# Layer 0 of a two-layer trunk: inverting the blocks of a head pair in one pass of eight instead of two passes of four

## The chip, the core and the metric

The kernel runs on one core of a Trainium2 chip. The metric is the device time of one execution in microseconds. The engines of the core are named as in the profile: PE (TensorE, matrix products; its weight loads are listed apart as PEld), DVE (VectorE), ACT (ScalarE), POOL (GpSimd) and SP, which here only issues transfers. Each engine runs its own list of instructions in order. PE alone writes PSUM, and DVE and ACT empty it.

## The reference

A trunk of two layers on 512 tokens of width 1024, in float32. Layer 0 mixes the tokens by two recurrent mixers, layer 1 by block attention. Each layer then has an MLP of width 4096 and a gated addition of a second input. The change lies in the second recurrent mixer of layer 0, which has 8 heads of width 64:

```python
def rwkv7_scan(r, decay, k, v, kk, a):
    def step(state, inp):
        r_t, w_t, k_t, v_t, kk_t, a_t = inp
        sa = jnp.einsum('bhvk,bhk->bhv', state, -kk_t)
        state = (state * w_t[:, :, None, :]
                 + sa[..., None] * (kk_t * a_t)[:, :, None, :]
                 + v_t[..., None] * k_t[:, :, None, :])
        return state, jnp.einsum('bhvk,bhk->bhv', state, r_t)
```

Beside it stands a gated linear recurrence with 4 heads of width 128 (`hgrn2_chunked`: scores inside chunks with decays, a state between chunks). The outputs of both are normalised, gated, joined and multiplied by `w_out`:

```python
    o = jnp.concatenate([o_a, o_b], axis=-1).astype(h.dtype)
    return o @ w_out
```

## The kernel before, in words

Large products are made to near float32 precision from three products of split operands: a weight tile of 128x512 is copied to a rounded upper half (`whi`, ACT, L230) and a remainder (`wlo`, DVE, L231), the activations likewise, and `mm3` issues three matmuls of 128x512 (L238 to L240) for each 128 rows of the sum. These are most of the work of PE, and their PSUM tiles come from the ring `pj` with two buffers. Small products of the recurrent mixers use the rings `pmr` (four buffers) and `pmh` (two).

The mixer of layer 0 goes over four head pairs h of the delta-rule mixer (called RWKV here) and, with the same index, four heads of the gated recurrence (HGRN). For each h the steps run in the order of `ORDER = "AFHBOC"`, by which the program is written; a scheduler then places each engine's instructions, the earliest written first among those that it takes for ready. Steps run by `run` get priority as if written 300 instructions earlier. The matmuls of later steps that are ready fill PE while a chain of small steps waits.

RWKV handles the 512 tokens of a head pair in two halves g of 256 tokens, and each half as four blocks (two groups of 128 tokens by two heads):

- `pre` (per pair): decays, normalised keys, the rows that the products need.
- `p1(h, g)`: triangular products of keys with keys and queries, and transposes.
- `p2(h, g)`: inverse of four unit-triangular blocks of 128 by doubling. Each of five levels is: a product of `n16` with the lower part of `X` (L658), a copy of it from PSUM by ACT to `PP` (L661), two products with `PP` (L658), and two masked copies by DVE into `X` (L663) and `XT` (L664). Then comes one correction step in float32 (L670 to L679) and a product with the values to `MU` (L684, L687).
- `p3(h, g)`: the matrices that carry the state over a chunk (L701 to L712), two products with 64 output rows (L720 and L725), the states one after another (L738, L740) and what they add to the output (L748).
- `tail(h)`: layer norm of the pair's output and its split (`os`).

Step A weaves `p2(h, 0)` with `p3(h-1, 1)`, `p1(h, 1)` and `tail(h-1)`; step C weaves `p2(h, 1)` with `pre(h+1)` and `p3(h, 0)` and then runs `p1(h+1, 0)`. `weave(main, side, ratio)` takes `ratio` steps of the side for each of the main.

HGRN (step H) has, for each head, score products over decays at six levels (L825, then five at L845, each behind a difference on POOL, L837, two exponentials on ACT and two products on DVE, L840 and L841), transposes of the keys (L862), products for the states (L867), the output (L876, L878), its mean square (L285), a reciprocal root in twelve small DVE instructions, its broadcast by PE (L328), and a gate, after which POOL (L892) and ACT (L271) make `os`. Step O multiplies the outputs of head h-1 by their part of `w_out` and adds them to `x` (L935). After the last head this is done for head 3, whose result `x` is scaled and split (`act`, L274 and L275) for the MLP of layer 0. The mean square of `x` is summed by POOL from squares made by ACT (`acc`, `xsq`, L307 and L313).

```python
        for h in range(4):
            for c in ORDER:
                step(c, h)
        out_piece(3)
```

Of the kernel before, what the change touches and what calls it, by code (L numbers as in the profile page):

```python
# [12 lines left out]
F32 = mybir.dt.float32  # L13
F32R = mybir.dt.float32r
F16 = mybir.dt.float16
# [15 lines left out]
ND = (2, 2)  # L31
PD = 1
ORDER = "AFHBOC"
R0, R1 = 1.5, 1.5
OFS = 300
NWARM = 9

P = 128
S = 512
# [140 lines left out]
def trunk(ctx, tc, wts, xT, pT, vecs, lora, cst, lev, seg, rope, out, upto="all", dbg=None, mode=None):  # L180
# [119 lines left out]
    class NormAcc:  # L300
# [1 line left out]
            self.ring, self.t = ring, None  # L302

        def add(self, src, eng="act"):
            sq = nrm.tile([P, S], F32, name="acc") if self.t is None else self.ring()
            if eng == "act":
                A.activation(sq, src, AF.Square)  # L307
            else:
                V.tensor_mul(sq, src, src)
            if self.t is None:  # L310
                self.t = sq
            else:
                G.tensor_add(self.t, self.t, sq)  # L313
# [27 lines left out]
    def weave(main, side, ratio):  # L341
        acc = 0.0
        for _ in main:
            yield
            acc += ratio
            while acc >= 1:
                acc -= 1
                if next(side, 0) is None:
                    yield
        for _ in side:  # L350
            yield

    def chain(*gens):
        for g_ in gens:
            yield from g_


    def layer0_mixer(actp):
# [5 lines left out]
        BZ = [mp.tile([P, 2, 2, 2, P], F32, name=f"BZ{i}") for i in range(2)]  # L364
        GB = mp.tile([P, 4, P], F32, name="GB")
        SB = mp.tile([P, 9, P], F32, name="SB")
        PP = mp.tile([P, 4, P], F16, name="PP")
        early = [BH, KAs, *NAs, *BZ, GB, SB, PP]
        for t in early[:NE]:
            G.memset(t, 0.0)  # L370
# [84 lines left out]
        def E(name="e", bufs=EB, shape=None, dt=F32):  # L455
            return ex.tile(shape or [P, S], dt, name=name, bufs=bufs)
# [53 lines left out]
        def four(lhs, rhs):  # L510
            ps = pmr.tile([P, S], F32, name="pmr")
            for i in range(4):
                T.matmul(ps[:, i * P:i * P + P], lhs(i), rhs(i), start=True, stop=True)
            return ps.rearrange("p (i t) -> p i t", i=4)
# [111 lines left out]
            A.copy(y[:, gs], ps[:, :256])  # L626
            yield

        def p2(hp, g):
            NA, TOK = un[hp, g]  # L630

            n16 = E("n16", 1, [P, 4, P], F16)
            for a in range(2):
                A.copy(n16[:, 2 * a:2 * a + 2, :], NA[:, a, :, 0, :])
            X = E("X", 1, [P, 4, P], F16)
            XT = E("XT", 1, [P, 4, P], F16)
            V.tensor_copy(XT, id16[:, None, :].to_broadcast([P, 4, P]))
            V.copy_predicated(XT[:, :, 1::2], m8[:, 0, None, 1::2].to_broadcast([P, 4, 64]), n16[:, :, 1::2])
            A.copy(X, four(lambda i: XT[:, i, :], lambda i: id16))
            yield  # L640
            for l in range(1, 6):
                H = 1 << l

                def lo(t):
                    return t.rearrange("p i (n u) -> p i n u", u=2 * H)[:, :, :, :H]

                def hi(t):
                    return t.rearrange("p i (n u) -> p i n u", u=2 * H)[:, :, :, H:]

                def mask(i, half):  # L650
                    m = half(m8[:, i:i + 1, :])
                    return m.to_broadcast([P, 4, 64 // H, H])

                def half4(lhs, rhs):
                    ps = pmr.tile([P, S], F32, name="pmr")
                    pv = ps[:, :256].rearrange("p (i n u) -> p i n u", i=4, u=H)
                    for i in range(4):
                        T.matmul(pv[:, i], lhs[:, i, :], rhs[:, i], start=True, stop=True)  # L658
                    return pv

                A.copy(lo(PP), half4(n16, lo(X)))  # L661
                yield
                V.copy_predicated(lo(X), mask(7 + l, lo), half4(XT, lo(PP)))  # L663
                V.copy_predicated(hi(XT), mask(l, hi), half4(PP, hi(XT)))  # L664
                yield
            tt = E("tt", 1, [P, 4, P])
            A.copy(tt, X)
            ps = pmr.tile([P, S], F32, name="pmr")
            for i, (a, h) in enumerate(pk):
                T.matmul(ps[:, i * P:i * P + P], NA[:, a, h, 0, :], tt[:, i, :], start=True, stop=False)  # L670
                T.matmul(ps[:, i * P:i * P + P], id16, id16, start=False, stop=True)
            er = E("er", 1, [P, 4, P], F16)
            V.tensor_sub(er, ps.rearrange("p (i t) -> p i t", i=4), tt)
            yield
            ps = pmr.tile([P, S], F32, name="pmr")
            for i in range(4):
                T.matmul(ps[:, i * P:i * P + P], er[:, i, :], XT[:, i, :], start=True, stop=False)
                T.matmul(ps[:, i * P:i * P + P], id16, XT[:, i, :], start=False, stop=True)
            A.copy(tt, ps.rearrange("p (i t) -> p i t", i=4))  # L679
            yield  # L680

            ps = pmr.tile([P, S], F32, name="pmr")
            for i, (a, h) in enumerate(pk):
                T.matmul(ps[:, i * P:i * P + P].rearrange("p (x f) -> p x f", x=2), tt[:, i, :],  # L684
                         TOK[a][:, 0::2, hs[h]], start=True, stop=True)
            MU = E("MU", 2, [P, 2, 2, P])
            A.copy(MU.rearrange("p a x (h f) -> p a h x f", h=2),  # L687
                   ps.rearrange("p (a h x f) -> p a h x f", a=2, h=2, x=2))
            un[hp, g] = (NA, TOK, MU)
            yield  # L690

        def p3(hp, g):
            lw, bh, kh, ar, rh_, bo, dl, v, y = pre_[hp]
# [86 lines left out]
        def run(*gens):  # L780
            with tc.high_priority(offset=OFS):
                for g_ in gens:
                    for _ in g_:
                        pass
# [119 lines left out]
        t = {}  # L904
# [35 lines left out]
        def pre_h(h):  # L940
            return pre(h, t["r", h], t["k", h], t["v", h])
# [20 lines left out]
        c2 = mp.tile([P, 4], F32, name="c2")  # L962
        V.tensor_scalar(c2, lb, -0.5, 0.5, op0=OP.mult, op1=OP.add)

        run(pre_h(0), p1(0, 0))
        def step(c, h):
            if c == "A":
                side = [p3(h - 1, 1)] if h else []
                side.append(p1(h, 1))
                if h:  # L970
                    side.append(tail(h - 1))
                run(weave(p2(h, 0), chain(*side), R0))
            elif c == "B":
                if h < 3:
                    proj_rkv(h + 1)
            elif c == "C":
                if h < 3:
                    run(weave(p2(h, 1), weave(pre_h(h + 1), p3(h, 0), 1), R1))
                    run(p1(h + 1, 0))
                else:  # L980
                    run(weave(p2(h, 1), p3(h, 0), R1))
                    run(p3(3, 1), tail(3))
            elif c == "F":
                for nm in "fqi":
                    proj_h(nm, h)
            elif c == "H":
                hgrn(h, t["q", h], t["f", h], t["i", h], lambda: proj_h("g", h))
            elif c == "O" and h:
                out_piece(h - 1)
# [332 lines left out]
```

## Time and profile before

| what | value |
|---|---|
| median of 3 runs | 1516.76 us (1516.53 to 1517.05) |
| the profiled execution's own time | 1517.83 us |
| its span, first to last instruction | 1516.0 us |
| mean granted TensorE clock | 0.997 |
| PE busy | 1489.2 us, 98% |
| DVE, ACT, POOL busy | 934.0, 657.0, 138.9 us |

The profile is of one execution, and busy time of PE counts matmuls to their modelled ends, so a matmul of 128x512 that starts 0.23 us after its forerunner is listed with 0.39 us. A granted clock of 1.0 is the 2.4 GHz level, 0.5 the 1.2 GHz level. In brackets at the end of a row of the timeline stands the idle time of the engine before the instruction and what ended it. Times along the span are microseconds from its first instruction.

### The profile page before, as it was taken

Reading aid. Unit: us, or ns where it says so; the run is one execution under the profiler, and the core shown is the slowest. Engines: PE = TensorE matmul, PEld = TensorE weight load, DVE = VectorE, ACT = ScalarE, POOL = GpSimd, SP = SyncE. Lnnn points to the kernel's source line nnn. Section 1 sums busy time; section 2 is a strip of 40 time slices with the busy share of each in tenths; the row PEclk is TensorE's granted clock in tenths of the full one; section 3 lists DMA queues with packets and bytes.
Section 4 is the critical chain, followed back from the end, with each engine's and each line's share of the span. In section 5 each row is a group of like instructions: output and inputs, shape, how many; then the busy total and the mean of one; then the engine's idle time right before and its main releaser. Section 6 shows DMA issues by size and latency. Waiting matters only on the chain.

```text
span 1516.0 us, 20763 instructions
## 1 busy us (share of the span) xinstructions
PE 1489.2 (98%) x7674; PEld 1205.7 (80%) x7674; DVE 934.0 (62%) x1859; ACT 657.0 (43%) x1277; POOL 138.9 (9%) x133
## 2 busy tenths in 40 slices
PE   8999999999999999999999999999999999999998
PEld 6778787777677788888888888777788888888887
DVE  6878697687785744444446637777565444445463
ACT  4575555554446433333334533444634333333342
POOL 4121220310205000000000200000320000000000
PEclk9999999999999999999999999999999999999999
DMA  5110111201123233333333332111222333333331
GB/s 179 56 36 22 55 46 44 63 29 50 35 91 111 84 98 97 98 98 97 98 98 98 120 111 81 54 54 49 77 91 91 98 103 95 98 96 97 98 98 70
DMA packets 66966, 123.64 MB, mean 82 GB/s; under 512 B 7616, under 2 KB 8000, under 8 KB 66864
## 3 DMA queue, kind: packets, MB, share of 16 engines
q1 hardware_dynamic: 65376, 118.57, 25.6%
q10 hardware_dynamic: 1008, 2.16, 0.5%
q0 software_dynamic: 480, 1.57, 0.3%
q8 instruction: 60, 0.98, 0.3%
q14 instruction: 42, 0.34, 0.1%
HBM read 120.18 MB, written 2.10 MB: 81 GB/s over the span
## 4 chain that ended last, share of the span: by engine, by line
PE 69%; DVE 1%; DMA 0%; issue 0%; ACT 0%; ACTq 0%; DVEq 0%
PE pj L238 19%; PE pj L240 19%; PE pj L239 19%; PE pmr L1213 1%; PE pmr L1237 1%; PE pmh L285 1%; PE pmr L239 1%; PE pmr L240 1%; PE pmr L238 1%; PE pmr L1230 1%; PE pmh L238 0%; PE pmr L1253 0%; PE pmh L240 0%; PE pmh L239 0%; PE pmr L1255 0%; PE pmr L1254 0%
## 5 line engine op out<-in xcount | busy, mean ns | idle before, releaser
L230 ACT CAST whi<-wr 128x512 fp32r<-128x512 f32 x428 | 265.1, 622 | 574.5 <-PE pj L239 472.1
L231 DVE TENSOR_TENSOR wlo<-wr,whi 128x512 fp32r<-128x512 f32 x428 | 311.6, 730 | 208.0 <-ACT whi L230 192.4
L238 PE MATMUL pj<-act,whi 128*128 128x512 f32 (+1 forms) x968 | 383.5, 397 | 1.0 <-DVE h L924 1.0
L239 PE MATMUL pj<-act,whi 128*128 128x512 f32 (+1 forms) x968 | 381.9, 395 | 0.0
L240 PE MATMUL pj<-act,wlo 128*128 128x512 f32 (+1 forms) x968 | 381.2, 395 | 0.5 <-DVE wlo L231 0.5
L238 PEld LDWEIGHTS pj<-act,whi 128*128 128x128 f32 x968 | 182.5, 189 | 38.0 <-ACT k L485 1.4
L240 PEld LDWEIGHTS pj<-act,wlo 128*128 128x128 f32 x968 | 182.6, 189 | 36.7 <-DVE wlo L231 1.5
L239 PEld LDWEIGHTS pj<-act,whi 128*128 128x128 f32 x968 | 182.6, 189 | 35.3 <-issue 1.7
L238 PE MATMUL pj<-hid,whi 128*128 128x512 f32 x512 | 199.4, 389 | 1.3 <-DVE x L1103 1.3
L240 PE MATMUL pj<-hid,wlo 128*128 128x512 f32 x512 | 199.2, 389 | 0.0
L239 PE MATMUL pj<-hid,whi 128*128 128x512 f32 x512 | 199.2, 389 | 0.0
L1103 DVE TENSOR_TENSOR x<-x,pj 128x512 f32<-128x512 f32 x128 | 87.9, 687 | 79.6 <-PE pj L240 79.2
L238 PEld LDWEIGHTS pj<-hid,whi 128*128 128x128 f32 x512 | 96.1, 188 | 21.5 <-DVE x L1103 1.7
L239 PEld LDWEIGHTS pj<-hid,whi 128*128 128x128 f32 x512 | 96.1, 188 | 20.1
L240 PEld LDWEIGHTS pj<-hid,wlo 128*128 128x128 f32 x512 | 96.1, 188 | 20.0
L313 POOL TENSOR_TENSOR acc<-acc,xsq 128x512 f32<-128x512 f32 x35 | 49.7, 1420 | 635.5 <-ACT xsq L307 616.5
L1092 DVE SCALAR_TENSOR_TENSOR r<-pj,rb 128x512 f32<-128x512 f32 x56 | 38.7, 691 | 86.2 <-PE pj L240 86.2
L272 DVE TENSOR_TENSOR hid<-r,hid 128x512 fp32r<-128x512 f32 x64 | 44.3, 692 | 42.3 <-ACT hid L271 42.3
L1093 ACT ACTIVATE r<-r 128x512 f32<-128x512 f32 x64 | 40.5, 632 | 21.1 <-DVE r L1092 21.0
L271 ACT CAST hid<-r 128x512 fp32r<-128x512 f32 x64 | 39.8, 621 | 1.9
L274 ACT ACTIVATE act<-x,vec 128x512 fp32r<-128x512 f32 x32 | 23.0, 720 | 27.2 <-DVE x L1121 12.7
L239 PE MATMUL pmr<-act,whi 128*128 128x512 f32 x80 | 32.2, 402 | 2.2 <-DVE act L275 2.2
(421 smaller groups left out, 2039.9 us busy)
## 6 DMA issues: line engine op xcount, KB each, us to landing
wr<-in_wts_dram SPq DMA_DIRECT2D x428, 256.0 KB, 2.7
x<-in_xT_dram SPq DMA_DIRECT2D x8, 256.0 KB, 6.7
sr<-in_wts_dram SPq DMA_DIRECT2D x8, 256.0 KB, 5.4
out_dram<-x SPq DMA_DIRECT2D x7, 256.0 KB, 2.0
r<-in_pT_dram ACTq DMA_DIRECT2D x4, 256.0 KB, 2.6
lw<-in_lora_dram POOLq DMA_DIRECT2D x4, 192.0 KB, 3.2
tqn<-in_rope_dram ACTq DMA_DIRECT2D x1, 512.0 KB, 5.8
tkn<-in_rope_dram ACTq DMA_DIRECT2D x1, 512.0 KB, 6.3
```

Source lines behind the costliest of these rows:

```text
L230: A.copy(hi, raw)
L231: V.tensor_sub(lo, raw, hi.bitcast(F32))
L238: T.matmul(ps, wh, xh, start=first, stop=False)
L239: T.matmul(ps, wh, xl, start=False, stop=False)
L240: T.matmul(ps, wl, xh, start=False, stop=last)
L271: A.copy(h, src)
L272: V.tensor_sub(l, src, h.bitcast(F32))
L274: A.activation(h, src, AF.Copy, scale=scale)
L313: G.tensor_add(self.t, self.t, sq)
L1092: V.scalar_tensor_tensor(r, q, 0.0, nf[0], op0=OP.max, op1=OP.mult)
L1093: A.activation(r, r, AF.Square)
L1103: V.tensor_add(x[k], x[k], ps)
```

## The change

`p2` loses its argument g and inverts all eight blocks of a head pair together: its tiles `n16`, `X`, `XT`, `PP` and `tt` hold 8 blocks, so ACT and DVE do one instruction of twice the size where there were two, and PE runs eight small products in a row instead of four. The correction and the products to `MU` still go by halves, one half behind the other, with one PSUM tile each. `p1` of both halves now stands before `p2`, and `p3` of both halves behind it. Step A is `p2(h)` woven with `tail(h-1)`, step C is both `p3` woven with `pre(h+1)`, then both `p1(h+1)`. The ratios of the weaves are 0.5 and 0.6 instead of 1.5. The accumulator `acc` of squares moves from a pool of its own to the pool `tmp`, which lies where tiles of the mixer were. In the changed file lines below the change are numbered 2 to 5 higher (L725, L730 for L720, L725; L743 for L738; L830, L850 for L825, L845; L940 for L935).

```diff
-R0, R1 = 1.5, 1.5
+R0, R1 = 0.5, 0.6
...
-            sq = nrm.tile([P, S], F32, name="acc") if self.t is None else self.ring()
+            sq = tmp.tile([P, S], F32, name="acc", bufs=1) if self.t is None else self.ring()
...
-        PP = mp.tile([P, 4, P], F16, name="PP")
+        PP = mp.tile([P, 8, P], F16, name="PP")
...
-        def p2(hp, g):
-            NA, TOK = un[hp, g]
+        def p2(hp):
...
-                def half4(lhs, rhs):
+                def half8(lhs, rhs):
                     ps = pmr.tile([P, S], F32, name="pmr")
-                    pv = ps[:, :256].rearrange("p (i n u) -> p i n u", i=4, u=H)
-                    for i in range(4):
+                    pv = ps.rearrange("p (i n u) -> p i n u", i=8, u=H)
+                    for i in range(8):
                         T.matmul(pv[:, i], lhs[:, i, :], rhs[:, i], start=True, stop=True)
                     return pv
 
-                A.copy(lo(PP), half4(n16, lo(X)))
+                A.copy(lo(PP), half8(n16, lo(X)))
                 yield
-                V.copy_predicated(lo(X), mask(7 + l, lo), half4(XT, lo(PP)))
-                V.copy_predicated(hi(XT), mask(l, hi), half4(PP, hi(XT)))
+                V.copy_predicated(lo(X), mask(7 + l, lo), half8(XT, lo(PP)))
+                V.copy_predicated(hi(XT), mask(l, hi), half8(PP, hi(XT)))
                 yield
...
+            for g in range(2):
+                ps = pmr.tile([P, S], F32, name="pmr")
+                for i, (a, h) in enumerate(pk):
+                    T.matmul(ps[:, i * P:i * P + P], NAs[g][:, a, h, 0, :], tt[:, 4 * g + i, :], start=True, stop=False)
+                    T.matmul(ps[:, i * P:i * P + P], id16, id16, start=False, stop=True)
+                gs = slice(4 * g, 4 * g + 4)
+                V.tensor_sub(er[:, gs, :], ps.rearrange("p (i t) -> p i t", i=4), tt[:, gs, :])
+                yield
...
-        run(pre_h(0), p1(0, 0))
+        run(pre_h(0), p1(0, 0), p1(0, 1))
+
         def step(c, h):
             if c == "A":
-                side = [p3(h - 1, 1)] if h else []
-                side.append(p1(h, 1))
-                if h:
-                    side.append(tail(h - 1))
-                run(weave(p2(h, 0), chain(*side), R0))
+                run(weave(p2(h), tail(h - 1), R0) if h else p2(h))
...
                 if h < 3:
-                    run(weave(p2(h, 1), weave(pre_h(h + 1), p3(h, 0), 1), R1))
-                    run(p1(h + 1, 0))
+                    run(weave(chain(p3(h, 0), p3(h, 1)), pre_h(h + 1), R1))
+                    run(p1(h + 1, 0), p1(h + 1, 1))
                 else:
-                    run(weave(p2(h, 1), p3(h, 0), R1))
-                    run(p3(3, 1), tail(3))
+                    run(p3(h, 0), p3(h, 1), tail(h))
```

What the scheduler makes of it is seen in the order of the engines. On PE, at the states of the last head pair's second half (NA_106 is that half's tile), the order before has:

```order
L705 MATMUL pmr<-TOK,BZ_109 128x128
L738 MATMUL pmr<-SB,GB 128x128
L720 MATMUL pmr<-NA_106,MU 64x128 x4
L867 MATMUL pmh<-vt,h 128x128 x2
L738 MATMUL pmr<-SB,GB 128x128
L725 MATMUL pmr<-NA_106,MU 64x128 x4
```

and the order of the changed kernel has at the same products (L725 is what was L720):

```order
L238 MATMUL pj<-act,whi 128x512
L239 MATMUL pj<-act,whi 128x512
L725 MATMUL pmr<-NA_106,MU 64x128
L240 MATMUL pj<-act,wlo 128x512
L725 MATMUL pmr<-NA_106,MU 64x128
L238 MATMUL pj<-act,whi 128x512
L725 MATMUL pmr<-NA_106,MU 64x128
L239 MATMUL pj<-act,whi 128x512
L725 MATMUL pmr<-NA_106,MU 64x128
L240 MATMUL pj<-act,wlo 128x512
L743 MATMUL pmr<-SB,GB 128x128
L730 MATMUL pmr<-NA_106,MU 64x128 x4
```

The four products with 64 output rows, which stood in a row, now alternate with projection matmuls. On PE at the HGRN scores of head 3 (KS0 and KS1 are the buffers of the level's keys, id16 and tt belong to the correction of `p2`), the order before has:

```order
L825 MATMUL pmh_4232<-h_4225,h_4226 128x128 x4
L845 MATMUL pmh_4245<-qs_4238,KS0_393 128x64 x4
L239 MATMUL pj_4422<-os_3278,whi_4412 128x512
L670 MATMUL pmr_4659<-tt_4657,NA1_106 128x128
L671 LDWEIGHTS id16_91
L671 MATMUL pmr_4659<-id16_91 128x128
L670 MATMUL pmr_4659<-tt_4657,NA1_106 128x128
L671 LDWEIGHTS id16_91
L671 MATMUL pmr_4659<-id16_91 128x128
```

and the changed one has the first levels of the same head as follows (L850 is what was L845; L328 and L779 belong to `tail(3)`):

```order
L830 MATMUL pmh_4205<-h_4198,h_4199 128x128 x4
L850 MATMUL pmh_4218<-qs_4211,KS0_393 128x64 x4
L240 MATMUL pj_4395<-os_3290,wlo_4386 128x512
L238 MATMUL pj_4395<-os_3980,whi_4391 128x512
L239 MATMUL pj_4395<-os_3981,whi_4391 128x512
L240 MATMUL pj_4395<-os_3980,wlo_4392 128x512
L850 MATMUL pmh_4231<-qs_4224,KS1_394 128x64 x4
L850 MATMUL pmh_4244<-qs_4237,KS0_393 128x64 x3
L328 MATMUL pmr_4608<-cs_85,bc_4609 128x128 x4
L779 MATMUL pmr_4617<-sg_392,lw_3533 128x512
L850 MATMUL pmh_4244<-qs_4237,KS0_393 128x64
L850 MATMUL pmh_4257<-qs_4250,KS1_394 128x64 x4
```

The inverse and states of head pair 3, which stood between the score levels, are gone from there, and the levels stand close together. On DVE, behind the split of head 3's outputs (os, L272) at the end of the mixer, the order before is:

```order
L272 TENSOR_TENSOR os_4407<-h_4333,os_4406 128x512
L231 TENSOR_TENSOR wlo_4970<-wr_4967,whi_4969 128x512
L272 TENSOR_TENSOR os_4781<-e_4746,os_4780 128x512
L231 TENSOR_TENSOR wlo_5007<-wr_5004,whi_5006 128x512
L231 TENSOR_TENSOR wlo_5064<-wr_5061,whi_5063 128x512
L935 TENSOR_TENSOR x0_76<-x0_76,pj_4796 128x512
L935 TENSOR_TENSOR x1_77<-x1_77,pj_4808 128x512
```

and in the changed kernel:

```order
L272 TENSOR_TENSOR os_4380<-h_4306,os_4379 128x512
L231 TENSOR_TENSOR wlo_4687<-wr_4684,whi_4686 128x512
L272 TENSOR_TENSOR os_4621<-e_4586,os_4620 128x512
L940 TENSOR_TENSOR x0_76<-x0_76,pj_4636 128x512
L940 TENSOR_TENSOR x1_77<-x1_77,pj_4648 128x512
L275 SCALAR_TENSOR_TENSOR act_4645<-x0_76,vec_84,act_4644 128x512
L275 SCALAR_TENSOR_TENSOR act_4657<-x1_77,vec_84,act_4656 128x512
```

Between the first `os` remainder and the last `act` remainder DVE has eight remainders of weights (L231) before and three now; the other five moved ahead of it.

## Rows read from the trace of the kernel before

**Rows 1.** The page, part 1: busy us, share of the span, instructions.

```profile
PE 1489.2 (98%) x7674; PEld 1205.7 (80%) x7674; DVE 934.0 (62%) x1859; ACT 657.0 (43%) x1277; POOL 138.9 (9%) x133
```

**Rows 2.** Busy time by stretch: stretch, length, engines, granted clock, DMA share, GB/s.

```profile
60.00:395.00 335.00, 328.57 (x2348) 259.92 (x2347) 252.72 (x607) 181.79 (x414) 57.29 (x58) 1.00 0.14 43
395.00:470.00 75.00, 67.50 (x374) 53.08 (x373) 59.50 (x126) 37.62 (x73) 20.54 (x16) 0.95 0.25 77
470.00:1517.00 1047.00, 1040.54 (x4733) 852.54 (x4731) 578.27 (x1037) 406.96 (x739) 39.71 (x28) 1.00 0.30 91
```

**Rows 3.** Waits of PE: line, what ended them, us in total, times, longest us.

```profile
PE pmr L239 <- DVE act L275: 3.0, 2, 2.2
PE pj L238 <- ACT os L271: 2.7, 1, 2.7
...
PE pmr L658 <- DVE X L663: 1.1, 3, 0.4
PE pmr L658 <- ACT PP L661: 1.1, 2, 0.7
```

**Rows 4.** Groups by form, 66 to 437: busy us, mean ns, idle before.

```profile
L663 DVE CAST_PREDICATED X<-m,pmr 128x256 f16<-128x256 uint8 x40 | 17.2, 431 | 11.5 <-PE pmr L658 11.0
L661 ACT CAST PP<-pmr 128x256 f16<-128x256 f32 x40 | 14.8, 370 | 32.4 <-PE pmr L658 32.3
L639 ACT CAST X<-pmr 128x512 f16<-128x512 f32 x8 | 4.7, 585 | 3.4 <-PE pmr L513 3.4
L826 DVE COPY_PREDICATED at<-m,pmh 128x512 f32<-128x512 uint8 x4 | 2.9, 730 | 0.0
```

**Rows 5.** Timeline of PE at a level of p2: start, us, instruction.

```profile
394.66 0.39 PE L238 MATMUL pj<-act,whi 128*128 128x512 f32 x1
394.89 0.39 PE L239 MATMUL pj<-act,whi 128*128 128x512 f32 x1
...
395.59 0.47 PE L238 MATMUL pj<-act,whi 128*128 128x512 f32 x1
395.90 0.40 PE L239 MATMUL pj<-act,whi 128*128 128x512 f32 x1
```

**Rows 6.** Timeline of PE at L720, alternating (378) and in a row (415).

```profile
378.28 0.43 PE L720 MATMUL pmr<-NA,MU 128*64 128x128 f32 x2
...
381.34 0.20 PE L658 MATMUL pmr<-X,n 128*128 128x64 f16 x1
...
415.10 0.66 PE L720 MATMUL pmr<-NA,MU 128*64 128x128 f32 x8
415.69 0.71 PE L867 MATMUL pmh<-vt,h 128*128 128x128 f32 x4
```

**Rows 7.** Weight loads of the projections, from the page's groups: busy us, mean ns.

```profile
L238 PEld LDWEIGHTS pj<-act,whi 128*128 128x128 f32 x968 | 182.5, 189 | 38.0 <-ACT k L485 1.4
```

**Rows 8.** Timeline of PE, score levels of head 3.

```profile
399.44 1.16 PE L825 MATMUL pmh<-h 128*128 128x128 f32 x8 [0.27 <-DVE h L820]
400.44 1.00 PE L845 MATMUL pmh<-qs,KS 128*128 128x64 f32 x8
...
403.96 1.08 PE L845 MATMUL pmh<-qs,KS 128*128 128x64 f32 x8 [0.44 <-DVE KS L841]
...
409.37 1.08 PE L845 MATMUL pmh<-qs,KS 128*128 128x64 f32 x8 [0.40 <-DVE eb L858]
```

**Rows 9.** Timeline of PE, broadcast of head 3 and long gaps.

```profile
433.67 0.60 PE L328 MATMUL pmh<-cs,rs_on 128*128 128x128 f32 x4
...
437.46 0.72 PE L238 MATMUL pj<-os,whi 128*128 128x512 f32 x2 [2.72 <-ACT os L271]
...
459.08 0.80 PE L239 MATMUL pmr<-act,whi 128*128 128x512 f32 x1 [2.19 <-DVE act L275]
```

**Rows 10.** Timeline of POOL behind the mixer.

```profile
455.51 10.45 POOL L313 TENSOR_TENSOR acc<-acc,xsq 128x512 f32<-128x512 f32 x7 [18.75 <-ACT xsq L307]
```

More of the change, by code (lines that the diff above doesn't have):

```diff
@@ L627, in p1 @@
             yield
-        def p2(hp, g):
-            NA, TOK = un[hp, g]
[L632 to L639, printed above, removed]
+        def p2(hp):
+            n16 = E("n16", 1, [P, 8, P], F16)
+            for g in range(2):
+                A.copy(n16[:, 4 * g:4 * g + 4, :].rearrange("p (a h) t -> p a h t", a=2), NAs[g][:, :, :, 0, :])
+            X = E("X", 1, [P, 8, P], F16)
+            XT = E("XT", 1, [P, 8, P], F16)
+            V.tensor_copy(XT, id16[:, None, :].to_broadcast([P, 8, P]))
+            V.copy_predicated(XT[:, :, 1::2], m8[:, 0, None, 1::2].to_broadcast([P, 8, 64]), n16[:, :, 1::2])
+            for g in range(2):
+                A.copy(X[:, 4 * g:4 * g + 4, :], four(lambda i: XT[:, 4 * g + i, :], lambda i: id16))
             yield
@@ L651, in mask @@
                     m = half(m8[:, i:i + 1, :])
-                    return m.to_broadcast([P, 4, 64 // H, H])
-                def half4(lhs, rhs):
+                    return m.to_broadcast([P, 8, 64 // H, H])
+                def half8(lhs, rhs):
                     ps = pmr.tile([P, S], F32, name="pmr")
-                    pv = ps[:, :256].rearrange("p (i n u) -> p i n u", i=4, u=H)
-                    for i in range(4):
+                    pv = ps.rearrange("p (i n u) -> p i n u", i=8, u=H)
+                    for i in range(8):
@@ L665, in p2 @@
                 yield
-            tt = E("tt", 1, [P, 4, P])
+            tt = E("tt", 1, [P, 8, P])
             A.copy(tt, X)
[L668 to L690, printed above, removed]
+            er = E("n16", 1, [P, 8, P], F16)
+            for g in range(2):
+                ps = pmr.tile([P, S], F32, name="pmr")
[5 more added lines that the diff above has]
+                yield
@@ new lines, in p2 @@
+            for g in range(2):
+                ps = pmr.tile([P, S], F32, name="pmr")
+                for i in range(4):
+                    T.matmul(ps[:, i * P:i * P + P], er[:, 4 * g + i, :], XT[:, 4 * g + i, :], start=True, stop=False)
+                    T.matmul(ps[:, i * P:i * P + P], id16, XT[:, 4 * g + i, :], start=False, stop=True)
+                A.copy(tt[:, 4 * g:4 * g + 4, :], ps.rearrange("p (i t) -> p i t", i=4))
+                yield
+            for g in range(2):
+                NA, TOK = un[hp, g]
+                ps = pmr.tile([P, S], F32, name="pmr")
+                for i, (a, h) in enumerate(pk):
+                    T.matmul(ps[:, i * P:i * P + P].rearrange("p (x f) -> p x f", x=2), tt[:, 4 * g + i, :],
+                             TOK[a][:, 0::2, hs[h]], start=True, stop=True)
+                MU = E("MU", 2, [P, 2, 2, P])
+                A.copy(MU.rearrange("p a x (h f) -> p a h x f", h=2),
+                       ps.rearrange("p (a h x f) -> p a h x f", a=2, h=2, x=2))
+                un[hp, g] = (NA, TOK, MU)
+                yield
```

## The prediction

> **What bounds the kernel now.** I read the busy times first, then the stretches, the waits of PE, and the timelines where PE waits. PE is busy for 1489.2 of 1516.0 us and DVE for 62% [rows 1]. The reader should see that no other engine comes near, so an instruction less on DVE or ACT is worth only what PE waits for it. The stretches say where PE idles: 6.4 us between 60 and 395 (335.00 less 328.57), where three and a half head pairs are worked off, 7.5 us between 395 and 470, where the mixer ends and the MLP begins, and 6.5 us in all the 1047 us behind [rows 2]. All that the change can win by shorter chains is thus below 14 us. The same rows give a granted clock of 0.95 in 395 to 470: 5% of 75 us is 3.7 us, and at half clock (the 1.2 GHz level) that is some 7 us run at half speed, about 3.4 us behind each of the two long gaps there, costing about 1.6 us each. The waits of PE by cause [rows 3]: the two great ones are not the inverse at all but the last `act` and the last `os`, 5.7 us together at the mixer's end. The levels of the inverse (X and PP) cost 2.2 us in five waits.
>
> The number of matmuls is the same before and after (480 in all at L658). So the prediction rests on three things: the waits of the levels, what the new order of PE costs in itself, and the end of the mixer. The counts come from the two orders, the durations from rows.
>
> **Levels of the inverse.** Removed: 20 of 40 copies to PP, 40 of 80 masked copies and half of the small setup copies. A masked copy of 256 columns takes 0.431 us, one of 512 in another step 0.730; a copy from PSUM by ACT takes 0.370 and 0.585 [rows 4]. DVE saves 80 x 0.43 less 40 x 0.73, about 5 us, and ACT 40 x 0.37 less 20 x 0.585, about 3 us. Neither is bound, so this counts nothing directly. What counts is that there are half as many hand-overs on which PE can be late, each later by 0.215 us (ACT) or 0.30 us (DVE). In the new order four projection matmuls (0.23 us each, [rows 5]) usually stand between the first product and the two with PP, 0.9 us against 0.585 plus the hand-over, and three matmuls plus the second group of eight between the two others. They cover it narrowly. I take half of the 2.2 us of [rows 3] as gone: -1.1. Bounds: -2.2 if all goes; if no level is covered any more, 20 levels x 0.515 = +10.3.
>
> **The order of PE in itself.** A projection matmul starts 0.23 us after its forerunner, but 0.31 us pass to the next start when a small product stood ahead of it (394.66 to 394.89, against 395.59 to 395.90) [rows 5]. So leaving the stream of projections and coming back costs 0.08 us. Up to the last output product of head 3, the stream is left 194 times before and 169 times after. But products with 64 output rows alternate with projections more often: six groups of four stand so after (one of pair 1, two of pair 2, three of pair 3), two before (both of pair 3). What this costs is in the trace [rows 6]: from 378.28 to 381.34 four pairs take 3.06 us. In a row the four products take 0.59 us (415.10 to 415.69), and four projections 4 x 0.23 plus 0.08, together 1.6. So each group more costs 1.45 us, four more 5.8 us. Those four groups hold 12 of the departures, so the other departures fall by 25 + 12 = 37, worth -3.0. Sum: +2.8. Bounds: -3.0 if the alternating groups lie where PE would have had to wait anyway, +5.8 if the fewer departures win nothing because the weight loads are exposed elsewhere.
>
> Here a rule of the Trainium skill may be weighed. The rows show a weight load of 0.189 us [rows 7] and an extra of 0.08 us per return, so more than half of the load is hidden even there. The page "TensorE: Matmul & The Clock Gate" of the Trainium skill, section "The mechanism", says that a weight load overlaps with matmuls in flight only when its group of rows differs. All these loads fill all 128 rows, so by it each departure would cost a whole load; the trace disagrees, since projections with such loads follow at 0.23 us. By the row the 37 departures are worth 3.0 us, by that rule 37 x 0.189 = 7.0 us, which makes it a rival below.
>
> **The end of the mixer, five terms.**
>
> First, the score levels of head 3. Before, PE idled 1.6 us in five gaps of 0.16 to 0.44 us there (first and last in [rows 8]), though the inverse and the states of pair 3 stood between the levels. Now only six projection matmuls (1.5 us), a broadcast and one product of `tail(3)` stand there. By the order DVE has some 10.7 us of work between the first score product and the last level's keys: nine products of about 0.41, four masked copies of 0.43, one of 0.73, five full-width instructions of about 0.68, eight tiny ones; this price is an estimate, from [rows 4] for the masked copies and 0.68 for the full width. PE has 0.93 + 4 x 0.9 + 1.5 + 1.35 = 7.4 us. It waits for the 3.3 us between. Cost +1.7. No further projections can fill in, because both buffers of `pj` are held, one by the gate projection whose emptying stands behind this chain on DVE. Bounds: -1.6 if DVE is ahead when PE arrives; +6.0 if the levels follow at the 3.5 us of the first two (400.44 to 403.96, [rows 8]) instead of about 2.5.
>
> Second, from the key transposes to the broadcast of head 3 PE had `p3(3, 1)` and `tail(3)` as cover and did not wait. Now 37 projections stand there, and DVE does two more weight remainders early. I take +1.8; bounds 0 and +4.6 (all of the cover that is missing: one 512-column product, three projections and the states' 3 us).
>
> Third, the wait for `os`, 2.72 us [rows 9]. Between the broadcast and the first product with `os` stand five projections instead of two (-0.7), and on DVE no weight remainder stands ahead of the scaling any more (-0.6): the gap becomes 1.4 us, -1.3. It is then shorter than either gap behind which the clock fell, so the half-speed stretch should go, -1.6. Bounds: 0 and -4.3.
>
> Fourth, the wait for the last `act`, 2.19 us [rows 9]. Three instead of eight weight remainders lie ahead of it on DVE (-3 us at 0.6), and 20 matmuls of the MLP stand between the last output product and the one that needs it. I take the gap as gone, -2.2, and its half-speed stretch too, -1.6. Bounds: 0 and -3.8.
>
> Fifth, the sum of squares. POOL's seven additions take 10.45 us [rows 10] and start when the first squares are done, which must wait for the memory of `os`. Now the accumulator lies in that memory as well, so two squares instead of one come first. PE reaches the statistics 47 matmuls behind the last output product, 11.0 us; the squares (two of about 0.62) and additions need about 12. Cost +1.0; bounds 0 and +1.7. What is queued behind that matmul on PE is the small product of the second input, and nothing else waits for it.
>
> Sum of the five: 1.7 + 1.8 - 2.9 - 3.8 + 1.0 = -2.2.
>
> **Sum.** -1.1 + 2.8 - 2.2 = -0.5 us. Against the profiled execution, 1517.83 us, this is 1517.3; that execution is 1.07 us above the median of the runs shown, so I forecast 1516.3 us. A change of this kernel below 0.2%, 3.0 us, cannot be told from none.
>
> **Rivals.**
>
> The alternation is free (faster). Where the 64-row products alternate, the states follow each other by hand-overs to DVE, and PE would have waited there. Then 5.8 us go from the sum: -6.3, 1510.5 us. For it: the scheduler alternates where chains are tight. Against it: PE idles only 6.4 us in 335, so it has little waiting to give. 0.26.
>
> Whole weight loads (faster). By the page's rule the departures are worth 4.0 us more: -4.5, 1512.3 us. Against it stand [rows 5]. 0.06.
>
> The score levels of head 3 become the chain (slower). If each level takes the 3.5 us of the first two in place of about 2.5, with PE out of filling work, this term is +6.0 instead of +1.7, and one of the gaps passes the length behind which the clock halved, +1.6: the sum is +5.4, 1522.2 us. It decides from about 3.2 us a level. For it: POOL's differences slow DVE there, and `tail(3)` now shares DVE with the levels. Against it: later levels were 1.5 to 2.1 us apart. 0.20.
>
> The merged levels are not covered (slower; the change then does not do what it says). Each of 20 levels exposes 0.515 us: +10.3 instead of -1.1, 1527.7 us. Against it: 0.9 us of projections stand between the steps. 0.06.
>
> **How the numbers follow.** My forecast has 0.42, the rivals 0.26, 0.06, 0.20 and 0.06. Faster by over 0.2%: 0.32. Slower: 0.26. Within: 0.42. The forecast's own range is 1513.8 to 1519.8. The range for 8 in 10 reaches to the first rival with some of its spread and to the third: 1510 to 1522.5.
>
> **What would show it.** Right on the levels: masked copies of about 0.73 us, 20 of each kind, and waits of PE for X and PP of about 1 us in all. Right on the order: PE's busy time in 60 to 395 no shorter, and 0.36 us from a lone 64-row product to the next start. Right on the end: the `os` gap about 1.4 us with a clock of 1.0 behind it, no gap before the last `act`, gaps of 3 us in the score levels, and about 1 us before the statistics. It is wrong if the `os` gap stays above 2 us, if score gaps exceed 6 us, or if the middle loses or wins more than 3 us.

## The result, and the profile after

The changed kernel takes 1534.26 us (1533.27 to 1535.08), the kernel before 1516.90 us beside it: a ratio of 1.0107, 95% interval 1.0092 to 1.0122. That is 17 us slower, outside the range given. The profiled execution took 1535.08 us, its span is 1533.3 us.

The busy times of the page, the counterpart of [rows 1], and the three stretches that answer to [rows 2] (stretch, length, busy time of PE, PEld, DVE, ACT and POOL, granted clock, DMA share, GB/s):

```profile
PE 1498.3 (98%) x7674; PEld 1214.2 (79%) x7674; DVE 931.0 (61%) x1811; ACT 653.3 (43%) x1245; POOL 140.5 (9%) x133
```

```profile
60.00:400.00 340.00, 328.54 (x2357) 261.84 (x2356) 246.02 (x557) 175.53 (x381) 58.03 (x58) 0.98 0.14 41
400.00:490.00 90.00, 80.34 (x381) 62.51 (x380) 64.60 (x135) 43.07 (x81) 22.68 (x17) 0.92 0.25 76
490.00:1534.00 1044.00, 1037.79 (x4721) 850.38 (x4719) 577.49 (x1032) 404.44 (x734) 38.45 (x28) 1.00 0.30 91
```

PE has as many matmuls as before, yet is busy 9.1 us longer and idle 8.2 us longer (35.0 against 26.8), together the 17.3 us of span. The longer busy time is the clock. The same view, cut at the stretches of half clock (the 1.2 GHz level):

```profile
124.87:138.52 13.65, 12.72 (x53) 10.19 (x54) 7.14 (x17) 3.51 (x13) 1.28 (x2) 0.50 0.01 1
428.66:432.07 3.41, 3.41 (x12) 2.71 (x13) 2.44 (x6) 1.33 (x3) 2.29 (x2) 0.50 0.00 0
435.49:438.90 3.41, 3.27 (x15) 2.76 (x15) 0.85 (x2) 0.48 (x1) 0.00 (x0) 0.50 0.38 113
455.96:459.37 3.41, 3.31 (x9) 2.54 (x9) 1.34 (x3) 0.00 (x0) 0.00 (x0) 0.50 0.48 150
483.27:486.68 3.41, 3.41 (x9) 2.48 (x8) 3.20 (x12) 1.69 (x3) 0.00 (x0) 0.50 0.71 225
```

They make 27.3 us, and PE is busy for 26.1 of it; before there were three stretches of 10.2 us, busy for 9.8. Half of the busy time in them is what the clock cost: 13.1 us against 4.9, so 8.2 us are lost. That leaves 0.9 us of busy time for the new order of PE itself. The waits of PE (line, what ended them, us in total, times, longest) have new names at the top compared with [rows 3]:

```profile
PE pmr L743 <- DVE GB L713: 4.3, 3, 3.3
PE pmh L850 <- DVE ra_ln L262: 2.2, 1, 2.2
PE pmh L850 <- DVE KS L846: 1.9, 2, 1.3
PE pmr L328 <- DVE bc L324: 1.8, 1, 1.8
PE pmh L285 <- POOL acc L313: 1.7, 1, 1.7
PE pj L238 <- ACT os L271: 1.7, 1, 1.7
```

**Head pair 0, second half of the states: 9.7 us.** PE's timeline (start, us, instruction, idle time before it and what ended it):

```profile
122.12 0.33 PE L850 MATMUL pmh<-qs,KS 128*128 128x64 f32 x2
125.80 0.80 PE L743 MATMUL pmr<-SB,GB 128*128 128x128 f32 x2 [3.35 <-DVE GB L713]
126.39 1.06 PE L328 MATMUL pmr<-cs,bc 128*128 128x128 f32 x4
127.38 1.12 PE L725 MATMUL pmr<-NA,MU 128*64 128x128 f32 x8
```

PE stands 3.35 us before the first state of the second half. The clock halves from 124.87, while PE still waits, to 138.52; PE is busy 12.72 us of that, which costs it 6.4 us. It waits for two copies to `GB`, one for each head of the pair; the second ends at 125.74. DVE's timeline shows what stood ahead of these copies, and POOL's what ran at the same time:

```profile
116.05 0.58 DVE L258 TENSOR_SCALAR ra_kk<-m_kk 128x8 int32<-128x8 int32 x1
...
117.80 0.90 DVE L263 SCALAR_TENSOR_TENSOR rs_kk<-ra_kk,rs_kk 128x8 f32<-128x8 f32 x1
...
118.97 0.47 DVE L262 SCALAR_TENSOR_TENSOR ra_kk<-ra_kk,m_kk 128x8 f32<-128x8 f32 x1
...
119.68 1.14 DVE L261 TENSOR_TENSOR ra_kk<-rs_kk 128x8 f32<-128x8 f32 x1
120.73 0.42 DVE L568 TENSOR_SCALAR bh<-bh 128x512 f32<-128x512 f32 x1
121.07 1.23 DVE L262 SCALAR_TENSOR_TENSOR ra_kk<-ra_kk,m_kk 128x8 f32<-128x8 f32 x1
...
124.39 0.28 DVE L713 TENSOR_TENSOR GB<-pmr,cs 64x128 f32<-64x128 f32 x1
124.67 0.75 DVE L486 SCALAR_TENSOR_TENSOR v<-u,vec,v 128x511 f32<-128x511 f32 x1
125.45 0.29 DVE L713 TENSOR_TENSOR GB<-pmr,cs 64x128 f32<-64x128 f32 x1
```

```profile
115.43 1.18 POOL L565 TENSOR_TENSOR ar<-r,pd 128x512 f32<-128x512 f32 x1
117.63 1.04 POOL L858 TENSOR_TENSOR h<-h 128x512 f32<-128x512 f32 x1 [1.02 <-DVE ra_kk L261]
118.67 0.76 POOL L547 TENSOR_SCALAR kh<-bh,vech,kah 128x512 f32<-128x512 f32 x1
119.51 1.28 POOL L548 TENSOR_TENSOR kh<-kh,k 128x512 f32<-128x512 f32 x1
120.75 1.52 POOL L860 TENSOR_TENSOR h<-h 128x512 f32<-128x512 f32 x1
```

The reciprocal root of pair 1's preparation, twelve tiny instructions, is queued ahead of the copies. In the kernel before the same root ran while POOL was idle, whose last instruction ahead of it ended at 106.20, and the root's instructions took 0.17 us each. This is POOL's timeline there, then the group view of DVE from 106.4 to 109.1 (busy us, mean ns):

```profile
105.02 1.18 POOL L565 TENSOR_TENSOR ar<-r,pd 128x512 f32<-128x512 f32 x1
```

```profile
L261 DVE TENSOR_TENSOR ra_kk<-rs_kk 128x8 f32<-128x8 f32 x3 | 0.5, 167 | 0.1
L262 DVE SCALAR_TENSOR_TENSOR ra_kk<-ra_kk,m_kk 128x8 f32<-128x8 f32 x3 | 0.5, 166 | 0.1
```

Now five of them end where an instruction of POOL ends (the two longest: 119.68 + 1.14 = 120.82 against 119.51 + 1.28 = 120.79; 121.07 + 1.23 = 122.30 against 120.75 + 1.52 = 122.27). Over the root they lose 3.5 us. The page "SBUF — State Buffer" of the Trainium skill, section "SBUF: two separate sides", says that VectorE with two inputs in SBUF, or in one of its two-port modes, and GpSimd exclude each other for a whole instruction. The trace agrees for the four with two inputs in SBUF. The fifth, L258, has one input and was held too; by the page it would have to be in such a mode, which no run here shows. An instruction with an input from PSUM was not held: the one for `SB` (L745) took 0.28 us beside L565 of POOL, its usual time.

**The end of the mixer: 5.7 us.** Between 400 and 490 PE idles 9.7 us (7.5 before, between 395 and 470, [rows 2]), and it has four stretches of half clock there, 6.7 us lost, against two with 3.2. PE in the score levels of head 3, the counterpart of [rows 8]:

```profile
421.76 1.13 PE L830 MATMUL pmh<-h 128*128 128x128 f32 x8 [0.46 <-DVE ra_ln L262]
422.73 1.00 PE L850 MATMUL pmh<-qs,KS 128*128 128x64 f32 x8
...
426.91 1.08 PE L850 MATMUL pmh<-qs,KS 128*128 128x64 f32 x8 [2.21 <-DVE ra_ln L262]
428.59 1.45 PE L850 MATMUL pmh<-qs,KS 128*128 128x64 f32 x6 [0.60 <-DVE KS L846]
...
434.78 1.30 PE L850 MATMUL pmh<-qs,KS 128*128 128x64 f32 x8 [1.31 <-DVE KS L846]
```

Here too the root of a layer norm (`ra_ln`, of `tail(3)`) runs beside POOL's differences and loses 3.2 us. Waits of 1.67 us for `os` and 1.71 us for `acc` follow, each with half clock behind it; the wait for the last `act` of [rows 9] is gone.

### The profile page after: what moved, and what is told of

It is laid out like the page before. It is cut to its first block, busy times and chain, and to the rows that moved or that the text cites. A ratio compares the mean times of both kernels' runs of the same rounds, so it can differ in the third digit from the quotient of the medians.

```text
span 1533.3 us, 20671 instructions
## 1 busy us (share of the span) xinstructions
PE 1498.3 (98%) x7674; PEld 1214.2 (79%) x7674; DVE 931.0 (61%) x1811; ACT 653.3 (43%) x1245; POOL 140.5 (9%) x133
## 4 chain that ended last, share of the span: by engine, by line
PE 90%; DVE 5%; ACT 2%; issue 1%; POOL 1%; DMA 0%; SPq 0%; ACTq 0%; DVEq 0%; POOLq 0%
PE pj L238 22%; PE pj L240 22%; PE pj L239 22%; PE pmh L285 1%; PE pmr L239 1%; PE pmr L238 1%; PE pmr L240 1%; PE pmr L1238 1%; PE pmr L1214 1%; PE pmh L850 1%; PE pmr L658 1%; PE pmr L594 1%; DVE wlo L231 1%; POOL acc L313 1%; PE pmr L672 1%
## 5 line engine op out<-in xcount | busy, mean ns | idle before, releaser
L231 DVE TENSOR_TENSOR wlo<-wr,whi 128x512 fp32r<-128x512 f32 x428 | 313.7, 735 | 213.9 <-ACT whi L230 193.7
L272 DVE TENSOR_TENSOR hid<-r,hid 128x512 fp32r<-128x512 f32 x64 | 44.3, 692 | 42.3 <-ACT hid L271 42.1
L275 DVE SCALAR_TENSOR_TENSOR act<-x,vec,act 128x512 fp32r<-128x512 f32 x32 | 26.1, 831 | 9.8 <-ACT act L274 9.6
```

The lines of the kernel that those rows point to most:

```text
L231: V.tensor_sub(lo, raw, hi.bitcast(F32))
L272: V.tensor_sub(l, src, h.bitcast(F32))
L275: V.scalar_tensor_tensor(l, src, scale, h.bitcast(F32), op0=OP.mult, op1=OP.subtract)
```

## The experiments

Each was timed beside the kernel before on the same chip, so ratios are compared; "before" in brackets is that median.

**The merge undone, the order kept.** `p2` as before, once for each half:

```diff
-                run(weave(p2(h), tail(h - 1), R0) if h else p2(h))
+                two = chain(p2(h, 0), p2(h, 1))
+                run(weave(two, tail(h - 1), R0) if h else two)
```

> The inverse again in two passes of four blocks, everything else in the order of the changed kernel (first products of both halves, then both inverses, then both states). Theory A (the loss of 17 us sits in three places of the new order, where work that used to lie behind the inverse now meets other work, and the merged inverse itself costs nothing): 1534 us, within 1529 to 1540, since the three places are left as they are. Theory B (the merged inverse is what costs: each hand-over of eight blocks is longer and PE waits for it): below 1524 us.

1527.88 us (before 1517.58), ratio 1.0069 (1.0056 to 1.0081). A miss of both ranges, between the two theories: the new order alone costs 10 us, the merge some 6 us on top. The trace shows where: in pair 0 the same wait for `GB` is 1.62 us with no half clock, and the root there loses 1.5 us and not 3.5. The end of the mixer has nearly the waits of the changed kernel (2.19, 1.27, 1.67 and 1.71 us) and one stretch of 3.41 us at half clock more.

**The states of pair 0 first.**

```diff
-                    run(weave(chain(p3(h, 0), p3(h, 1)), pre_h(h + 1), R1))
+                    if h:
+                        run(weave(chain(p3(h, 0), p3(h, 1)), pre_h(h + 1), R1))
+                    else:
+                        run(p3(0, 0), p3(0, 1), pre_h(1))
```

> The changed kernel, but for head pair 0 both halves' states come ahead of the preparation of pair 1 instead of woven with it, so the reciprocal root of that preparation no longer stands ahead of the copies to GB on DVE. Theory A: the wait of 3.35 us for GB and the 13.65 us at half clock behind it go, 3.35 + 6.8 = 10.2 us at most; expected 1526 us (1523 to 1530), as some of the wait turns up where the preparation now ends later. Theory B: 1534 us.

1539.30 us (1517.58), 1.0146 (1.0132 to 1.0160): slower, a miss. Pair 0 does as expected (0.8 us of waits from 100 to 150, clock 1.0), but the preparation of pair 1 is late, and pair 1 pays, each time with 3.41 us at half clock behind it. The score levels of head 3, with the waits of the changed kernel, also have 13.65 us at half clock in place of 6.82.

```profile
217.89 0.80 PE L743 MATMUL pmr<-SB,GB 128*128 128x128 f32 x2 [3.26 <-DVE GB L713]
...
234.01 1.24 PE L594 MATMUL pmr<-ar,BH 128*128 128x128 f32 x8 [3.00 <-ACT BH L590]
```

**The tail of pair 3 later.**

```diff
-                    run(p3(h, 0), p3(h, 1), tail(h))
+                    run(p3(h, 0), p3(h, 1))
+                    for _ in tail(h): pass
```

> The changed kernel, but the tail of head pair 3 (layer norm with its reciprocal root) loses its priority and so comes behind the score levels of head 3 instead of among them. Theory A: the waits of 2.21, 0.60 and 1.31 us in the score levels shrink and the two stretches at half clock there (3.41 us each, 1.7 us of loss each) go, some of it paid back at the end of the tail: 1530 us (1527 to 1533). Rival: the levels wait for their own chain of POOL, ACT and DVE and not for the tail, and the tail is late at the end: 1535 to 1538 us.

1530.77 us (1517.58), 1.0088 (1.0074 to 1.0102). Within the range: the root loses nothing, the waits in the levels are 1.04 and 1.29 us, and the wait for `os` grows to 3.97 us. Only one of the two stretches of half clock is gone. Some luck is in it: up to the score levels PE's list is that of the changed kernel, yet the profiled execution has 10.24 us at half clock in pair 0 in place of 13.65, which the edit can't have made.

**Head 3's inputs earlier**, so that its levels fall among the states of pair 3. The second form also gives steps F of heads 0 to 2 an (empty) priority block, which moves pair 0:

```diff
-                    proj_h(nm, h)
+                    with tc.high_priority(offset=OFS): proj_h(nm, h)    # f3_early: h == 3 only
+                    with tc.high_priority(offset=OFS if h == 3 else 0): proj_h(nm, h)    # f3_early_v2
```

> The changed kernel, but the three projections of step F for head 3 get priority, so the HGRN scores of head 3 start earlier and the states of pair 3 stand between their levels again; up to head 2 nothing moves. Theory A (the score levels of head 3 cost because nothing stands between them on PE): the waits in the levels (2.21, 0.60, 1.31 us) fall below 2 us in all and the two stretches at half clock there go: 2 to 2.6 us plus 3.4 us, so 1528.5 us (1526 to 1531). Rival (the levels are late by their own chain on POOL, ACT and DVE, and the states only add work for DVE): 1532 us or more.

> The same priority for the projections of step F of head 3, written so that the place in the program of the steps F of heads 0 to 2 shifts too: now in head pair 0 the copies to GB stand between the steps of the reciprocal root on DVE instead of behind it, and nine projection matmuls stand ahead of the broadcast. Theory A: as for the other one at the end (5.5 us), and the wait of 3.35 us for GB falls below 1 us with no half clock behind it, up to 10 us: 1520 us (1517 to 1526). Theory C (what is taken off one place comes back at the next, since PE has no more filling work): within 2 us of the other one.

f3_early: 1521.63 us (1516.98), 1.0026 (1.0016 to 1.0036). f3_early_v2: 1513.46 us, 0.9975 (0.9964 to 0.9985). Both are faster than their ranges: f3_early was to win 5.5 us and won 12.6. PE in the levels, f3_early:

```profile
408.75 0.61 PE L830 MATMUL pmh<-h 128*128 128x128 f32 x4
409.19 0.78 PE L850 MATMUL pmh<-qs,KS 128*128 128x64 f32 x6
...
410.39 0.46 PE L743 MATMUL pmr<-SB,GB 128*128 128x128 f32 x2 [0.42 <-DVE GB L713]
410.78 0.66 PE L725 MATMUL pmr<-NA,MU 128*64 128x128 f32 x8
411.37 1.33 PE L850 MATMUL pmh<-qs,KS 128*128 128x64 f32 x10
```

States stand between the levels, the waits before L850 are gone, and there is no half clock after 400, so the stretches behind `os` and `acc`, on which the forecast didn't count, are gone too. The profiled execution (1519.50 us) is the fastest of the eight, and its pair 0 has 6.83 us at half clock. In f3_early pair 0 still waits 3.35 us, in f3_early_v2 0.62 us, and that is 8.2 us faster. The gains add: theory C falls.

**POOL's part.** Of the five POOL instructions beside the root, three (L547, L548 and L860) go to DVE:

```diff
+            E1 = V if hp == 1 else G
-            G.tensor_scalar(kh, bh, ...); G.tensor_mul(kh, kh, k)
+            E1.tensor_scalar(kh, bh, ...); E1.tensor_mul(kh, kh, k)
-            G.tensor_mul(d, d, k)
+            (G if h else V).tensor_mul(d, d, k)
```

> The changed kernel, but in head pair 0's second half three instructions of POOL go to DVE: the two products for kh of pair 1 and the product of head 0's keys. Theory P (the tiny instructions of the reciprocal root took up to 1.23 us instead of 0.17 because POOL's instructions ran at the same time, 3.5 us in all): the root's instructions take 0.17 us each but for one beside the difference on POOL that stays, GB comes 1.5 to 2 us sooner though DVE has three instructions more, the wait of 3.35 us falls to 1.5 us or less and the 13.65 us at half clock to 3.41 or none: 1527 us (1525 to 1531). Rival (GB is late because it is queued behind the root and the preparation, whoever does the products): the wait stays at 3 us or more, 1533 to 1536 us.

1524.84 us (1516.98), 1.0051 (1.0039 to 1.0064), 9.4 us less than the changed kernel and just below the range of theory P. DVE there (line numbers one higher):

```profile
117.87 0.17 DVE L262 SCALAR_TENSOR_TENSOR ra_kk<-ra_kk,m_kk 128x8 f32<-128x8 f32 x1
...
122.90 0.27 DVE L714 TENSOR_TENSOR GB<-pmr,cs 64x128 f32<-64x128 f32 x1
...
123.88 0.61 DVE L714 TENSOR_TENSOR GB<-pmr,cs 64x128 f32<-64x128 f32 x2
```

The root loses 0.4 us in place of 3.5, the two copies to `GB` come at 122.90 and 123.88 instead of 124.39 and 125.45 with more work on DVE, and the wait and the half clock are gone. One part isn't POOL's: the keys come earlier too, and 16 score matmuls instead of two cover PE from 122.40 to 124.23. How the 9.4 us divide between the two is not shown.

**Cures together, and controls.** f3_pool has both edits; before_f3 the priority alone in the kernel before; before_acc only the accumulator of the change in it. (The accumulator back in its own pool in the changed kernel, a run called acc_back, gave no time: beside the wider tiles memory is 1 KB per partition short, so with these pools that part of the change is forced.)

```diff
-            sq = nrm.tile([P, S], F32, name="acc") if self.t is None else self.ring()
+            sq = tmp.tile([P, S], F32, name="acc", bufs=1) if self.t is None else self.ring()    # before_acc
```

> The changed kernel with both cures together: the projections of step F of head 3 early, and in pair 0's second half the two products for kh and the product of head 0's keys on DVE instead of POOL. If the two losses are separate places (theory A), the gains add: 12.6 us (f3_early) and 9.4 us (pool_off) off 1534.3 us, 1512 us (1510 to 1515), below the kernel before. If the filling work is only shifted (theory C), 1517 us or more.

> The kernel before with the projections of step F of head 3 early, the control for f3_early: there the inverse of pair 3 already stands between the score levels, which wait 1.6 us in all. Theory A: little to win, 1517 us (1514 to 1519); then a gain of the merged kernels over before is the merge's. Theory D (early projections help any kernel by as much): 1508 us or less.

> The kernel before with only the accumulator of squares moved into the pool tmp. By the trace of before the last addition ends 0.4 us ahead of the statistics on PE; with two squares instead of one ahead of the additions they end later by about 1 us or up to 3 us. Expected 1518 us if no half clock follows (1517 to 1518.5), 1519 to 1520 if it does; unchanged if the place of the accumulator is not what makes it late.

f3_pool: 1514.29 us (1517.27), 0.9980 (0.9971 to 0.9989). before_f3: 1517.03 us, 0.9999 (0.9990 to 1.0008). before_acc: 1516.34 us, 0.9995 (0.9986 to 1.0004). The first two as expected. The third is a miss: PE does wait 2.15 us for `acc` there, but the wait for the last `act` is gone and the time is the same.

**The ratios of the weaves.**

```diff
-R0, R1 = 0.5, 0.6
+R0, R1 = 1.5, 1.5    # ratios_15, and order_r15 on order_alone; r1_15: 0.5, 1.5
```

> The changed kernel with the ratios of the two weaves at 1.5 again. The preparation of pair 1 then comes ahead of the states, its reciprocal root is done before the second half's copies to GB stand in line, and 20 projection matmuls and the transposes of HGRN stand between. Theory A: the wait of 3.35 us and the 13.65 us at half clock in pair 0 go or shrink, 5 to 10 us: 1526 us (1524 to 1530), the end as it was. If the states now come too late for the next pair's products, 1534 us or more.

> The changed kernel with only the ratio of step C (states against the preparation of the next pair) at 1.5, that of step A (inverse against the tail) left at 0.5. If the place of pair 0's states decides, as theory A has it: 1520 us (1518 to 1523). If the tail's place in step A is what costs: 1528 us or more.

> Two passes of four blocks, in the order of the changed kernel and with both ratios at 1.5: beside ratios_15 (1519.1 us) it has the inverse alone different. Theory A (the merged inverse costs nothing or wins a little): the same to 5 us slower, 1519 to 1525 us. Theory B (hand-overs of eight blocks cost): 1515 us or less.

ratios_15: 1519.10 us (1517.27), 1.0012 (1.0003 to 1.0020). r1_15: 1518.87 us (1517.84), 1.0014 (1.0004 to 1.0024). order_r15: 1523.49 us (1517.84), 1.0040 (1.0028 to 1.0052). ratios_15 is a miss, 5 us below its range; the other two are within theirs. So the ratio of step C alone makes some 15 of the 17 us: the root of the next pair's preparation, ahead of the states, is then done before the second half's copies queue. DVE in ratios_15, the root's last instruction and the first of those copies:

```profile
125.71 0.16 DVE L263 SCALAR_TENSOR_TENSOR rs_kk<-ra_kk,rs_kk 128x8 f32<-128x8 f32 x1
...
132.47 0.28 DVE L713 TENSOR_TENSOR GB<-pmr,cs 64x128 f32<-64x128 f32 x1
```

At this ratio the merge wins 4 us. ratios_15 gains more than the wait and half clock of pair 0, though: its busy time less what half clock added is 7 us below that of before, an effect of PE's order that I did not take apart.

**The best order, with and without the merge.** Head 3's inputs early: in two passes with the ratios of the changed kernel (order_f3_early), and with both ratios at 1.5 in one pass (r15_f3) and in two (order_r15_f3). The edits are those shown above:

> Two passes of four blocks in the new order, as in order_alone (1527.9 us), with the projections of step F of head 3 early. Theory A: the waits of 2.19 and 1.27 us in the score levels and the 6.83 and 3.41 us at half clock there go, 3 + 5 us: 1520.5 us (1518 to 1524). If the accumulator in the memory of os is what holds the end back, 1525 us or more.

> The changed kernel with both ratios at 1.5 and the projections of step F of head 3 early. In ratios_15 (1519.1 us) the waits in the score levels of head 3 (2.19 and 1.28 us) and the half clock there (6.83 and 3.41 us) were as in the changed kernel, so theory A: the gain of f3_early adds, 12.6 us off 1519.1: 1506.5 us (1504 to 1510), the fastest of all. Theory C (filling work is only shifted): 1513 us or more.

> Two passes of four blocks with both ratios at 1.5 and the projections of step F of head 3 early: r15_f3 (1509.1 us) with the merge alone undone. On PE the stream of projections is left 217 times instead of 175, 42 more, at 0.08 us some 3.4 us. Theory A (the merge wins by the order of PE): 1512 to 1516 us. If the merge is worth nothing in itself: within 2 us of 1509.

order_f3_early (two passes, ratios as changed): 1523.49 us (1516.98), 1.0042 (1.0029 to 1.0055), within the range, but a miss in the mechanism: the waits before the score levels are gone, and yet 13.65 us at half clock lie in them (399.79 to 413.44). r15_f3: 1509.11 us (1517.84), 0.9949 (0.9936 to 0.9961), as expected, the fastest, 8.7 us below before. order_r15_f3: 1518.84 us (1518.39), 1.0009 (0.9999 to 1.0020), slower than its range of 1512 to 1516. There the merge itself is worth 9 us; the lowest time of order_r15_f3, 1517.0 us, lies above the highest of r15_f3, 1512.8. By the two profiles, whose spans are 13.6 us apart, it isn't PE's order alone: that makes 5.8 us of busy time at full clock, and half clock another 6.8. The page of r15_f3:

```profile
PE 1476.8 (98%) x7674; PEld 1205.5 (80%) x7674; DVE 928.7 (62%) x1811; ACT 652.5 (43%) x1245; POOL 141.2 (9%) x133
```

PE is busy 12.4 us less than in [rows 1], with the same matmuls, and 1.5 us of that is the clock: the gain is in the order of PE, and its waits are longer than before (30.3 us idle).

## Why the prediction was wrong

**Levels of the inverse**, forecast -1.1 us: about 0. The copies came out as predicted (group view of DVE and ACT, 66 to 400):

```profile
L663 DVE CAST_PREDICATED X<-m,pmr 128x512 f16<-128x512 uint8 x20 | 14.1, 706 | 10.7 <-PE pmr L658 10.6
L661 ACT CAST PP<-pmr 128x512 f16<-128x512 f32 x20 | 11.7, 583 | 16.3 <-PE pmr L658 16.3
```

PE waits 2.0 us at L658 (2.2 before), 1.4 of it behind a key product of HGRN on DVE. The fourth rival (levels uncovered) is out.

**Order of PE**, +2.8: +0.9. The alternating groups are there, but one price per departure doesn't carry: by the order f3_early_v2 leaves the stream 191 times and ratios_15 192 times (252 for the whole kernel before), and their busy time less what half clock added differs by 4.4 us (1483.2 - 1.7 against 1485.2 - 8.1). The direction holds: r15_f3 leaves it 175 times and has 1473.4 us so counted, the kernel before 1484.3.

**End of the mixer**, -2.2: +5.7. The `act` wait went with its half clock as forecast (-3.7 for -3.8). The `os` wait fell to 1.67 us (forecast 1.4), but the half clock stayed: the step "It is then shorter than either gap behind which the clock fell, so the half-speed stretch should go" failed. The statistics waited 1.71 us (the bound) plus a stretch not counted, +3.4 for +1.0. From the key transposes to the broadcast PE waited 0.9 us more (forecast 1.8). The score levels were mis-sized: +3.0 of waits and +3.3 of clock for +1.7. DVE took 12.9 us from the first score product to the last level's keys (421.76 to 434.63) for the 10.7 estimated, and `tail(3)`'s root lost 3.2 us there beside POOL. This is the third rival's place and nearly its price (+6.0 and 1.6), but not by 3.5 us a level throughout.

**What no term held**: the wait in pair 0, +9.7. The failed step is "So the prediction rests on three things": it puts the waits between 60 and 395, other than those of the inverse, at nothing, without a reason. The sentence "All that the change can win by shorter chains is thus below 14 us" bounds a gain; no bound on a loss there, the inverse apart, was sought. The prediction walked the inverse and the end, and nowhere the states of pair 0, though there the order put the next preparation's root ahead of the copies to `GB`. The changed ratio of step C, which r1_15 shows to make most of the loss, has no term either, nor has what POOL does beside a root. That pair 0 suffers because no output product of an earlier pair stands by as filling is argued from the program and not shown; in states_first pair 1 waited nearly as long (3.26 us). One of the prediction's own signs came: "if the middle loses or wins more than 3 us".

The rest: waits in other places of 60 to 400 +1.7, the start -0.7 (waits 1.0 us longer, one stretch of half clock less). 0 + 0.9 + 5.7 + 9.7 + 1.7 - 0.7 = 17.3 us, the 17.3 us of span.

## What to carry to other kernels

When a change moves a chain out of the shadow of another, follow each engine's queue at the place it moves to, once for every round of the loop; here the losses lay in the first round and the last. An idle bound of PE limits what can be won, not what can be lost: a wait of 3.35 us cost 9.7 with the clock. The merge was worth 9 us in one order and cost 6 in another, so the weave's ratio is part of such a change and is tried with it.

## What the runs showed of the hardware

The price of a wait in clock isn't fixed by its length. The wait of 3.35 us in pair 0 came with 13.65 us at half clock in the profiled execution of the changed kernel, 10.24 in that of tail3_late and 6.83 in that of f3_early, though up to there PE's list is the same in all three. So a single profile doesn't give the price of a wait to better than some 3 us. A wait of 1.31 us in the changed kernel (434.78) had half clock behind it, one of 1.82 us (59.19) had not; the wait of 1.71 us for `acc` had it in the changed kernel and not in f3_early, where from 467.04 to 477 the clock is 1.00. In order_f3_early the clock halved at 399.79 with no wait above 0.90 us in the 10 us before. What decides was not settled.

Tiny instructions on DVE with two inputs in SBUF took up to 1.23 us instead of 0.17 beside an instruction of POOL, and a chain of twelve lost 3.5 us.
